# Gated copies of a token matrix: which partition holds which block of rows

## The chip, the cores and the metric

The kernel runs on one core of a Trainium2 chip. The metric is the device time in microseconds of one execution, as a median over runs. A profile of one further execution gives the engines' work in time.

## The reference

For each of 16 × 1024 = 16384 tokens there is a row `x` of 512 float32 values and 8 router logits. The two largest probabilities of the softmax over the logits are normalised to a sum of one, and the output holds the token's row twice, once scaled by each of the two (the smaller first).

```python
probs = np.exp(router_logits - logits_max)
probs = probs / np.sum(probs, axis=-1, keepdims=True)
topk_indices = np.argsort(probs, axis=-1)[..., -k:]
topk_probs = np.take_along_axis(probs, topk_indices, axis=-1)
topk_probs = topk_probs / np.sum(topk_probs, axis=-1, keepdims=True)
x_expanded = x[:, :, np.newaxis, :].repeat(k, axis=2)
return (x_expanded * topk_probs[..., np.newaxis]).astype(np.float32)
```

With two weights that sum to one, each is a sigmoid of the difference of the two largest logits. The input is 33.6 MB of `x` and 0.5 MB of logits, the output 67.1 MB.

## The kernel before

The 16384 tokens lie in 128 partitions, 128 tokens in each, in two groups: 65 tokens of each partition, then 63 (`GROUPS`). Within a group, partition p has the block of tokens 65p to 65p + 64 (or 63p to 63p + 62), which is contiguous in DRAM for `x`, for the logits and for the output. The views `x_v`, `o_v` and `rl_v` (lines 91 to 93) say so, with a rearrangement "(p m) d -> p m d".

`LOADS` says in which pieces a group's `x` is loaded into the tile `xs` (line 112): 6, 28 and 31 tokens of each partition for the first group, 32 and 31 for the second. The logits are loaded behind the first piece (lines 105 and 106), and `top2_weights` works out the weights `WA` of all tokens from them on VectorE and, for the sigmoids, ScalarE.

`STORES` is an order written out by hand. Each entry has the number of tokens of each partition, the place of the scaled rows, how many of the tokens ScalarE does, and the queue. The place is either in the tile `osp` or in `xs` itself, over tokens that have been used already. For each entry VectorE multiplies (line 127), for a few tokens ScalarE does (line 135), and one DMA stores the result (line 138). All loads and all stores but the first go through the SP queue; the first store, of two tokens, goes through ACT's. Sixteen DMAs are issued in all: five loads of `x`, two of logits, nine stores. A DMA moves one contiguous run for each partition, since a partition's tokens are neighbours in DRAM.

What waits for what follows from the tiles: a multiply waits for the load of its tokens, and for the store that last read the place it writes; a load of the second group waits for the stores that read from the same part of `xs`; a store waits for its multiply. The SP queue takes its DMAs in the order of the program, so a DMA that waits holds back those behind it.

Of the kernel before, what the change touches and what calls it, by code (L numbers as in the profile page):

```python
# [1 line left out]

# [4 lines left out]

F32 = mybir.dt.float32
ALU = mybir.AluOpType
ACTF = mybir.ActivationFunctionType  # L10
P = 128
E = 8
D = 512


GROUPS = [65, 63]
M = sum(GROUPS)


LOADS = [[6, 28, 31], [32, 31]]  # L20


STORES = [
    [
        (2, ("osp", 0), 0, "ACT"),
        (16, ("osp", 2), 0, "SP"),
        (16, ("x", 2), 0, "SP"),
        (16, ("osp", 0), 4, "SP"),
        (15, ("x", 35), 0, "SP"),
    ],  # L30
    [
        (16, ("osp", 0), 1, "SP"),
        (16, ("x", 0), 0, "SP"),
        (16, ("osp", 0), 4, "SP"),
        (15, ("x", 33), 0, "SP"),
    ],
]
OSP = 18


def top2_weights(nc, scratch, logits, WA):

    used = [0]

    def cut(n):
        a = scratch[:, used[0] : used[0] + M * n].rearrange("p (m n) -> p m n", n=n)
        used[0] += M * n
        return a

    a, b = logits[:, :, 0:4], logits[:, :, 4:8]  # L50
    hi = cut(4)
    lo = b
    nc.vector.tensor_tensor(hi, a, b, op=ALU.max)  # L53
    nc.vector.tensor_tensor(lo, a, b, op=ALU.min)  # L54
    n = 4
    while n > 1:
        n //= 2
        a, b = hi[:, :, 0:n], hi[:, :, n : 2 * n]
        nhi, nlo, tmp = cut(n), cut(n), cut(n)
        nc.vector.tensor_tensor(tmp, lo[:, :, 0:n], lo[:, :, n : 2 * n], op=ALU.max)  # L60
        nc.vector.tensor_tensor(nlo, a, b, op=ALU.min)  # L61
        nc.vector.tensor_tensor(nlo, nlo, tmp, op=ALU.max)  # L62
        nc.vector.tensor_tensor(nhi, a, b, op=ALU.max)  # L63
        hi, lo = nhi, nlo
    dlt = cut(1)
    nc.vector.tensor_tensor(dlt, hi, lo, op=ALU.subtract)  # L66
    nc.scalar.activation(WA[:, :, 0], dlt[:, :, 0], ACTF.Sigmoid, scale=-1.0)  # L67
    nc.scalar.activation(WA[:, :, 1], dlt[:, :, 0], ACTF.Sigmoid, scale=1.0)  # L68


@with_exitstack
def kernel(
    ctx: ExitStack,
    tc: tile.TileContext,
    x: bass.AP,
    router_logits: bass.AP,
    k: bass.AP,
    out: bass.AP,
):
    nc = tc.nc  # L80
    N = x.shape[0] * x.shape[1]
    assert int(k) == 2 and router_logits.shape[-1] == E and x.shape[2] == D
    assert N == P * M
    xf = x.rearrange("b s d -> (b s) d")
    of = out.rearrange("b s k d -> (b s) k d")
    rf = router_logits.rearrange("b s e -> (b s) e")
    x_v, o_v, rl_v = [], [], []
    t0 = 0
    for n in GROUPS:
        t1 = t0 + P * n  # L90
        x_v.append(xf[t0:t1].rearrange("(p m) d -> p m d", p=P))
        o_v.append(of[t0:t1].rearrange("(p m) k d -> p m k d", p=P))
        rl_v.append(rf[t0:t1].rearrange("(p m) e -> p m e", p=P))
        t0 = t1

    pool = ctx.enter_context(tc.tile_pool(name="pool", bufs=1))
    xs = pool.tile([P, max(GROUPS), D], F32)
    osp = pool.tile([P, OSP, 2, D], F32)
    WA = pool.tile([P, M, 2], F32)

    logits = osp[:, OSP - 1].rearrange("p k d -> p (k d)").rearrange("p (m e) -> p m e", e=E)
    scratch = osp[:, OSP - 3 : OSP - 1].rearrange("p r k d -> p (r k d)")

    def load_logits():
        nc.sync.dma_start(logits[:, : GROUPS[0]], rl_v[0])  # L105
        nc.sync.dma_start(logits[:, GROUPS[0] :], rl_v[1])  # L106

    m0 = 0
    for g, G in enumerate(GROUPS):
        r = 0  # L110
        for n in LOADS[g]:
            nc.sync.dma_start(xs[:, r : r + n, :], x_v[g][:, r : r + n, :])  # L112
            if g == 0 and r < 6 <= r + n:
                load_logits()
                top2_weights(nc, scratch, logits, WA)
            r += n
        assert r == G
        r = 0
        for n, (home, a), by_act, queue in STORES[g]:
            if home == "x":  # L120
                og = xs[:, a : a + 2 * n, :].rearrange("p (r k) d -> p r k d", k=2)
            else:
                og = osp[:, a : a + n]
            v = n - by_act
            w = WA[:, m0 + r : m0 + r + n, :]
            if v:
                nc.vector.tensor_tensor(  # L127
                    og[:, :v],
                    xs[:, r : r + v, :].unsqueeze(2).to_broadcast([P, v, 2, D]),
                    w[:, :v].unsqueeze(3).to_broadcast([P, v, 2, D]),  # L130
                    op=ALU.mult,
                )
            for i in range(v, n):
                for c in range(2):
                    nc.scalar.activation(  # L135
                        og[:, i, c], xs[:, r + i, :], ACTF.Copy, scale=w[:, i, c : c + 1]
                    )
            {"SP": nc.sync, "ACT": nc.scalar}[queue].dma_start(o_v[g][:, r : r + n], og)  # L138
            r += n
        assert r == G  # L140
        m0 += G


# [1 line left out]
_INS = ['x', 'router_logits', 'k']  # L145
_OUTS = [((16, 1024, 2, 512), 'float32')]

_NUMBERS = {'k': 2}


# [26 lines left out]
```

## Time and profile before

| | |
|---|---|
| median of 3 runs | 239.22 us (239.19 to 239.43) |
| profiled execution | 239.38 us, of which 237.6 us are its span (first to last instruction) |
| VectorE busy | 132.2 us |
| ScalarE busy | 13.2 us |
| moved by DMA | 101.19 MB, 426 GB/s over the span |

The profile's page gives busy times of the engines, a row of forty slices of the span with the mean busy share of the sixteen DMA engines in tenths, the DMA queues with their packets, the chain of work that ended last, and the DMAs that were issued with the time from issue to landing. A view by windows gives the DMA share and the rate of any stretch. "SPq" is the SP queue's sequencer, "L127" line 127 of the kernel. In a row such as `xs<-in_x_dram` the target stands to the left.

### The profile page before, as it was taken

The numbers are of one execution on the slowest core, as the hardware profiler recorded it, in microseconds if no ns is written. First come the engines' busy times: TensorE is split into PE (matmuls) and PEld (weight loads), VectorE is DVE, ScalarE is ACT, GpSimd is POOL, SyncE is SP. The second block draws the span as 40 slices with busy tenths as digits, with TensorE's granted clock in tenths as the row PEclk, the third lists the DMA queues.
The fourth block names the chain that finished last, engine by engine and source line by source line (L and its number), as shares of the span: only waits on it lengthen the run. The fifth ranks groups of instructions, "written<-read, shape, count | busy, mean of one in ns | idle before, by whom it ended". The sixth has DMA issues, their size and how long they took to land.

```text
span 237.6 us, 124 instructions
## 1 busy us (share of the span) xinstructions
DVE 132.2 (56%) x20; ACT 13.2 (6%) x21; POOL 0.2 (0%) x4
## 2 busy tenths in 40 slices
DVE  0640599999289999000000009999956999920000
ACT  2000000000080000000000001000006100000000
POOL 0000000000000000000000000000000000000000
DMA  7979989898989989899998989898989989897995
GB/s 265 541 338 488 408 386 535 348 530 353 496 386 441 441 353 530 353 508 414 414 519 353 508 370 502 353 519 353 496 386 419 463 353 530 353 530 342 496 445 217
DMA packets 2304, 101.19 MB, mean 426 GB/s; under 512 B 256, under 2 KB 384, under 8 KB 512
## 3 DMA queue, kind: packets, MB, share of 16 engines
q1 hardware_dynamic: 2160, 100.14, 97.7%
q10 hardware_dynamic: 144, 1.05, 1.0%
HBM read 34.08 MB, written 67.11 MB: 426 GB/s over the span
## 4 chain that ended last, share of the span: by engine, by line
DMA 48%; DVE 39%; SPq 1%; issue 0%; DVEq 0%
DMA xs<-in_x_dram 30%; DVE osp L127 25%; DMA out_dram<-osp 19%; DVE xs L127 14%; SPq L105 0%; SPq L106 0%; SPq L112 0%; SPq L138 0%; DVEq L127 0%
## 5 line engine op out<-in xcount | busy, mean ns | idle before, releaser
L127 DVE TENSOR_TENSOR osp<-xs,WA 128x12288 f32<-128x12288 f32 (+3 forms) x5 | 61.6, 12318 | 68.7 <-DMA xs<-in_x_dram 58.4
L127 DVE TENSOR_TENSOR xs<-xs,WA 128x16384 f32<-128x16384 f32 (+1 forms) x4 | 66.8, 16692 | 0.3
L135 ACT ACTIVATE osp<-xs,WA 128x512 f32<-128x512 f32 x18 | 11.4, 709 | 161.3 <-DMA out_dram<-osp 90.0
L53 DVE TENSOR_TENSOR osp<-osp 128x512 f32<-128x512 f32 x1 | 0.7, 692 | 8.2 <-DMA osp<-in_router_logits_dram 8.2
L67 ACT ACT_TABLE_LOAD x1 | 1.3, 1283 | 0.7 <-PEq L158 0.7
L67 ACT ACTIVATE WA<-osp 128x128 f32<-128x128 f32 x1 | 0.3, 316 | 10.1 <-DVE osp L66 10.1
L54 DVE TENSOR_TENSOR osp<-osp 128x512 f32<-128x512 f32 x1 | 0.7, 693 | 0.0
L60 DVE TENSOR_TENSOR osp<-osp 128x256 f32<-128x256 f32 (+1 forms) x2 | 0.7, 352 | 0.0
L62 DVE TENSOR_TENSOR osp<-osp 128x256 f32<-128x256 f32 (+1 forms) x2 | 0.7, 352 | 0.0
L63 DVE TENSOR_TENSOR osp<-osp 128x256 f32<-128x256 f32 (+1 forms) x2 | 0.7, 352 | 0.0
L61 DVE TENSOR_TENSOR osp<-osp 128x256 f32<-128x256 f32 (+1 forms) x2 | 0.7, 351 | 0.0
L66 DVE TENSOR_TENSOR osp<-osp 128x128 f32<-128x128 f32 x1 | 0.3, 292 | 0.0
L68 ACT ACTIVATE WA<-osp 128x128 f32<-128x128 f32 x1 | 0.3, 298 | 0.0
L158 POOL MEMSET const-bfloat16-1.0<- 128x1 bf16 x1 | 0.1, 102 | 0.0
L158 POOL MEMSET const-uint8-127<- 128x1 uint8 x1 | 0.1, 102 | 0.0
L158 POOL MEMSET const-float32-0.0<- 128x1 f32 x1 | 0.1, 99 | 0.2 <-issue 0.2
L158 POOL MEMSET const-float32-1.0<- 128x1 f32 x1 | 0.1, 99 | 0.0
## 6 DMA issues: line engine op xcount, KB each, us to landing
xs<-in_x_dram SPq DMA_DIRECT2D x2, 7936.0 KB, 40.8
out_dram<-xs SPq DMA_DIRECT2D x2, 7680.0 KB, 27.5
xs<-in_x_dram SPq DMA_DIRECT2D x1, 7168.0 KB, 24.2
xs<-in_x_dram SPq DMA_DIRECT2D x1, 1536.0 KB, 6.0
out_dram<-osp ACTq DMA_DIRECT2D x1, 1024.0 KB, 24.5
osp<-in_router_logits_dram SPq DMA_DIRECT2D x1, 260.0 KB, 6.2
osp<-in_router_logits_dram SPq DMA_DIRECT2D x1, 252.0 KB, 6.4
out_dram<-osp SPq DMA_DIRECT2D x4, 23.9
```

The costliest lines, as they stand in the source:

```text
L53: nc.vector.tensor_tensor(hi, a, b, op=ALU.max)
L54: nc.vector.tensor_tensor(lo, a, b, op=ALU.min)
L60: nc.vector.tensor_tensor(tmp, lo[:, :, 0:n], lo[:, :, n : 2 * n], op=ALU.max)
L61: nc.vector.tensor_tensor(nlo, a, b, op=ALU.min)
L62: nc.vector.tensor_tensor(nlo, nlo, tmp, op=ALU.max)
L63: nc.vector.tensor_tensor(nhi, a, b, op=ALU.max)
L66: nc.vector.tensor_tensor(dlt, hi, lo, op=ALU.subtract)
L67: nc.scalar.activation(WA[:, :, 0], dlt[:, :, 0], ACTF.Sigmoid, scale=-1.0)
L68: nc.scalar.activation(WA[:, :, 1], dlt[:, :, 0], ACTF.Sigmoid, scale=1.0)
L127: nc.vector.tensor_tensor(og[:, :v], xs[:, r : r + v, :].unsqueeze(2).to_broadcast([P, v, 2, D]), w[:, :v].unsqueeze(3).to_broadcast([P, v ...
L135: nc.scalar.activation(og[:, i, c], xs[:, r + i, :], ACTF.Copy, scale=w[:, i, c : c + 1])
L158: nc = _bacc.Bacc("TRN2", target_bir_lowering=False, num_devices=1)
```

## The change

The three views get one dimension more. With partition 64a + b (a of 0 or 1, b of 0 to 63), the partition now has block 2b + a of its group, where it had block 64a + b. Even blocks go to partitions 0 to 63, odd ones to 64 to 127. `x`, logits and output use the same assignment. The lines that use the views index one dimension more; tiles, pieces, queues and order stay. Lines behind 86 have numbers one higher than before.

```diff
-        x_v.append(xf[t0:t1].rearrange("(p m) d -> p m d", p=P))
-        o_v.append(of[t0:t1].rearrange("(p m) k d -> p m k d", p=P))
-        rl_v.append(rf[t0:t1].rearrange("(p m) e -> p m e", p=P))
+        x_v.append(xf[t0:t1].rearrange("(b a m) d -> a b m d", a=2, b=P // 2))
+        o_v.append(of[t0:t1].rearrange("(b a m) k d -> a b m k d", a=2, b=P // 2))
+        rl_v.append(rf[t0:t1].rearrange("(b a m) e -> a b m e", a=2, b=P // 2))
...
-            nc.sync.dma_start(xs[:, r : r + n, :], x_v[g][:, r : r + n, :])
+            nc.sync.dma_start(xs[:, r : r + n, :], x_v[g][:, :, r : r + n, :])
...
-            {"SP": nc.sync, "ACT": nc.scalar}[queue].dma_start(o_v[g][:, r : r + n], og)
+            {"SP": nc.sync, "ACT": nc.scalar}[queue].dma_start(o_v[g][:, :, r : r + n], og)
```

## The prediction

> **What bounds the kernel now.** I read the page first: the busy times, the DMA row of the forty slices, the packet count and the queues.
>
> ```profile
> span 237.6 us, 124 instructions
> ...
> DVE 132.2 (56%) x20; ACT 13.2 (6%) x21; POOL 0.2 (0%) x4
> ...
> DMA  7979989898989989899998989898989989897995
> ...
> DMA packets 2304, 101.19 MB, mean 426 GB/s; under 512 B 256, under 2 KB 384, under 8 KB 512
> ## 3 DMA queue, kind: packets, MB, share of 16 engines
> q1 hardware_dynamic: 2160, 100.14, 97.7%
> q10 hardware_dynamic: 144, 1.05, 1.0%
> HBM read 34.08 MB, written 67.11 MB: 426 GB/s over the span
> ```
>
> VectorE works 132.2 us of 237.6. The sixteen DMA engines are busy 97.7% + 1.0% = 98.7% of the span, from the first slice to the last, so the transfers set the time: about 0.987 × 237.6 = 234.5 us of work for each of the sixteen engines and 3.1 us in which they stand idle, at the start and behind the last landing. The view by windows gives the rate in stretches.
>
> ```profile
> 0.00:10.00 10.00, 1.81 (x4) 1.28 (x1) 0.20 (x4) 1.00 0.98 393
> 26.00:44.00 18.00, 17.61 (x2) 0.00 (x0) 0.00 (x0) 1.00 1.02 442
> 142.00:180.00 38.00, 33.38 (x2) 1.34 (x2) 0.00 (x0) 1.00 1.01 435
> ...
> 26.00:236.00 210.00, 126.07 (x8) 11.36 (x18) 0.00 (x0) 1.00 1.00 431
> ```
>
> The last two columns are the DMA share and GB/s. From 26 to 236 us all sixteen engines are always busy (1.00) and move 431 GB/s, 26.9 GB/s for each engine. The chain of waits is divided between DMA and VectorE:
>
> ```profile
> DMA 48%; DVE 39%; SPq 1%; issue 0%; DVEq 0%
> DMA xs<-in_x_dram 30%; DVE osp L127 25%; DMA out_dram<-osp 19%; DVE xs L127 14%; SPq L105 0%; SPq L106 0%; SPq L112 0%; SPq L138 0%; DVEq L127 0%
> ```
>
> Its 39% of VectorE isn't a second limit: a multiply is followed by its store, but other transfers fill the engines meanwhile, which the share of 1.00 shows.
>
> **How a transfer is spread now.** This is what the change touches. The list of DMA issues:
>
> ```profile
> xs<-in_x_dram SPq DMA_DIRECT2D x2, 7936.0 KB, 40.8
> out_dram<-xs SPq DMA_DIRECT2D x2, 7680.0 KB, 27.5
> xs<-in_x_dram SPq DMA_DIRECT2D x1, 7168.0 KB, 24.2
> xs<-in_x_dram SPq DMA_DIRECT2D x1, 1536.0 KB, 6.0
> out_dram<-osp ACTq DMA_DIRECT2D x1, 1024.0 KB, 24.5
> osp<-in_router_logits_dram SPq DMA_DIRECT2D x1, 260.0 KB, 6.2
> osp<-in_router_logits_dram SPq DMA_DIRECT2D x1, 252.0 KB, 6.4
> out_dram<-osp SPq DMA_DIRECT2D x4, 23.9
> out_dram<-xs SPq DMA_DIRECT2D x2, 24.1
> xs<-in_x_dram SPq DMA_DIRECT2D x1, 46.4
> ```
>
> These are 16 DMAs, and 2304 packets are 144 for each: 128 with data, one for each partition, and 16 more. The 256 packets under 512 B are the 16 × 16 small ones, since the shortest run of data is a partition's logits, 252 KB / 128 = 2016 B. I read the 16 as one completion for each engine that took part: every DMA was cut into 16 parts of 8 partitions.
>
> **The change part by part.** The instructions of both kernels stand in the same order on every engine; only the DMAs' patterns differ. One load and one store of each, DRAM side beside SBUF side, as they are built:
>
> ```
> before  load   x    [128][3072]          xs   [128][3072]
> after   load   x    [2][64][3072]        xs   [128][1][3072]
> before  store  out  [128][16384]         osp  [128][16384]
> after   store  out  [2][64][16384]       osp  [128][1][16384]
> ```
>
> Bytes, contiguous runs (one for each partition, 2016 B to 64 KB) and partitions stay as they are. No compute instruction is added, removed or moved, and no wait. In DRAM, partition 64a + b now steps two blocks for each b and one for a; the two steps can't be merged into one, so the outermost count on the DRAM side is 2 in all 16 DMAs. The unknown is into how many parts such a DMA is cut, and the trace, where both sides always begin with 128, has no row with another count. The bounds:
>
> - Sixteen parts as now: the 234.5 us for each engine stay, and the time is 239.38 us, that of the profiled execution.
> - Two parts, one for each value of the outermost count: the packets' time is 16 × 234.5 = 3752 engine-us, so 1876 us on each of two engines. By the rate it is the same: 101.19 MB / (2 × 26.9 GB/s) = 1880 us.
>
> I take two. In this trace the parts are equal and made of whole partitions (16 × 8 = 128), a cut along the first dimension of both patterns. With 2 on one side and 128 on the other, no more than two equal parts can be cut along both. For sixteen, the cut would have to go through the first dimension on the one side and the second on the other, and no row shows that it can.
>
> [...]
>
> The sum: 1876 us of packets, plus the same 3.1 us of idle start and end, is a span of 1879 us; plus 239.38 - 237.6 = 1.8 us around the span, 1881 us. The median of the runs, 239.22, is 0.16 us below the profiled execution, which doesn't matter here.
>
> This holds if the two engines never run dry. VectorE's work doesn't grow:
>
> ```profile
> L127 DVE TENSOR_TENSOR xs<-xs,WA 128x16384 f32<-128x16384 f32 x2 | 34.5, 17225 | 0.1
> ...
> L127 DVE TENSOR_TENSOR osp<-xs,WA 128x12288 f32<-128x12288 f32 x2 | 25.9, 12958 | 9.8 <-DMA out_dram<-osp 9.8
> ```
>
> A multiply takes at most 17.2 us, and each big transfer, at 53.9 GB/s, 136 us (7168 KB) to 156 us (a store of 16 rows, 8.39 MB). In each place where the kernel waits, one such transfer is still under way: the first big multiply waits for the 7168 KB load while the 7936 KB load follows; the third store's buffer waits for the second to land while the third is already queued (counting the small store as the first); the second group's first load is queued behind two stores, and its first multiply runs while its second load moves. That second load is the closest call, since SP holds it back until the last store of the first group has landed:
>
> ```profile
> SPq L112 <- DMA out_dram<-xs: 26.2, 1, 26.2
> ```
>
> It is issued when the first load of that group, ahead of it, has just begun, with some 156 us to go. So the waits become longer but stay covered: nothing is added. Were this cover gone, each of the eight big multiplies would add up to 17.2 us, 138 us in all.
>
> The issue is on the path once:
>
> ```profile
> 0.73 0.38 SPq L112
> ```
>
> A pattern of more dimensions may take longer to issue; no row shows by how much. Between 0 and a doubling that is up to 0.4 us at the start, and I take 0: the later issues stand in front of a full queue.
>
> **The rivals.**
>
> *Sixteen parts after all* (the change does nothing to the spread): this is the case that is not slower. [...] For it speaks that the partitions are still 128 and the parts can be made of the same 128 runs; against it, that the patterns no longer start alike. The time is 239.4 us. Other addresses then meet at the same moment in DRAM, to either side; with 3.1 us idle in all, a gain can't pass 1.3%, and there is no row from which to price a loss.
>
> *Two engines, each faster.* If the 26.9 GB/s were the share of a limit common to all sixteen, two alone could draw more. At twice the rate: 1876 / 2 + 4.9 = 943 us. Against it: the share is 1.00 with 431 GB/s over loads, stores and mixtures of both, which looks like an engine's own pace. No row has few engines at work.
>
> *One engine, or two in each other's way.* If the whole DMA went to one engine, or the two had to share a path, 3752 + 4.9 = 3757 us. For it speaks only that the trace never shows two engines alone; against it, that 2 divides both 2 and 128.
>
> **How the numbers follow.** Two engines at the present rate: 82%. Sixteen: 12%, of which 3% faster, 5% the same, 4% slower. Two engines clearly faster: 3%. One engine, or half the rate: 3%. The likeliest time is 1881 us. Its own bounds are rates that rows show: the fastest stretch, 442 GB/s, makes 101.19 MB / (442 / 8) + 4.9 = 1836 us; the first ten us, with 393 GB/s at a share of 0.98 (401 GB/s at full share, small and first packets among them), make 101.19 MB / (401 / 8) + 4.9 = 2024 us. The range of 1830 to 2025 us leaves out the other cases, 18% in all. A measurement of this kernel can tell about 0.2% from no change. Slower by more than that: 82 + 4 + 3 + 3 = 92%; within it 5%; faster 3%.
>
> **What would show it.** In the changed kernel's profile I expect a mean DMA share near 2/16 (0.12 to 0.13) through the span, about 54 GB/s, the same 101.19 MB, and 16 × (128 + 2) = 2080 packets, 32 of them under 512 B. The 7936 KB load would move in about 151 us when alone. VectorE's multiplies keep their 13.0 and 17.2 us, 132.2 us in sum, and idle between them grows; the chain becomes nearly all DMA. The forecast is wrong if the packets stay 2304 with a share near 0.99 (sixteen parts), if the share is 2/16 but the rate far from 54 GB/s (the pace isn't the engine's own), or if the share falls well under 2/16 in the middle of the span (the cover by queued transfers fails).

## The result

The changed kernel takes 1871.3 us (median of 4 runs, 1871.29 to 1871.57), the kernel before 239.2 us (239.16 to 239.43). The ratio is 7.818, with a 95% interval of 7.808 to 7.827. Here and below, a median and its range are of all runs of a kernel, and a ratio with an interval is of the runs within 1.5% of its fastest. The forecast was 1881 us, with a range of 1830 to 2025.

The page of the changed kernel, with the parts that were read of the kernel before (span, busy times, share of the DMA engines and GB/s in forty slices, packets, queues, and the chain that ended last):

```profile
span 1869.5 us, 124 instructions
## 1 busy us (share of the span) xinstructions
DVE 132.2 (7%) x20; ACT 13.2 (1%) x21; POOL 0.2 (0%) x4
...
DMA  1111111111111111111111111111111111111111
GB/s 50 55 54 56 54 54 54 55 53 53 56 53 53 56 53 53 56 54 55 53 55 56 53 53 54 54 54 56 53 53 56 53 55 55 53 56 53 55 53 53
DMA packets 2080, 101.19 MB, mean 54 GB/s; under 512 B 32, under 2 KB 160, under 8 KB 288
## 3 DMA queue, kind: packets, MB, share of 16 engines
q1 hardware_dynamic: 1950, 100.14, 12.4%
q10 hardware_dynamic: 130, 1.05, 0.1%
...
another core or an unknown queue 68%; DVE 7%; DMA 2%; SPq 0%; issue 0%; ACT 0%; DVEq 0%
```

The same 101.19 MB move and VectorE has the same 132.2 us, but the DMA row, which was 7 to 9 in all slices but the last, is 1 everywhere. The shares of 12.4% and 0.1% make 12.5%, which is two engines of sixteen, busy all the time. There are 32 small packets where there were 256: two completions for each of 16 DMAs. The chain can't put a name to its longest part, and the page's list of DMA issues has no times to landing for this run; that the profile can't match two completions to their DMA is a guess. The program has one core, so that these 68% are not another core's. The waits show what they are:

```profile
DVE osp L128 <- DMA xs<-in_x_dram: 725.8, 2, 579.2
...
DVE osp L128 <- DMA out_dram<-osp: 541.9, 2, 271.2
```

The first big multiply of each group waits for a load and the third for a store, at the same places as before (58.4 and 9.8 us in the kernel before). The two rows add up to 1267.7 us, which is 68% of the span.

### The profile page after: what moved, and what is told of

Same layout as the page of the kernel before. It is cut to its first block, busy times and chain, and to the rows that moved or that the text cites. A ratio compares the mean times of both kernels' runs of the same rounds, so it can differ in the third digit from the quotient of the medians.

```text
span 1869.5 us, 124 instructions
## 1 busy us (share of the span) xinstructions
DVE 132.2 (7%) x20; ACT 13.2 (1%) x21; POOL 0.2 (0%) x4
## 2 busy tenths in 40 slices
DMA packets 2080, 101.19 MB, mean 54 GB/s; under 512 B 32, under 2 KB 160, under 8 KB 288
## 3 DMA queue, kind: packets, MB, share of 16 engines
q1 hardware_dynamic: 1950, 100.14, 12.4%
## 4 chain that ended last, share of the span: by engine, by line
another core or an unknown queue 68%; DVE 7%; DMA 2%; SPq 0%; issue 0%; ACT 0%; DVEq 0%
DVE xs L128 4%; DVE osp L128 3%; DMA osp<-in_router_logits_dram 2%; DVE osp L53 0%; DVE osp L54 0%; SPq L113 0%; DVE osp L62 0%; DVE osp L63 0%; DVE osp L61 0%; DVE osp L60 0%; SPq L106 0%; ACT WA L67 0%; DVE osp L66 0%; ACT WA L68 0%
```

## The experiments

Two questions stood behind the forecast: does the outermost count of 2 alone do this, or does the new order of blocks in DRAM have a part in it; and is 27 GB/s an engine's own pace, so that the number of engines is all that matters?

### The new assignment without the 2

Each DMA is issued as two, one for each a, with 64 partitions on both sides:

```diff
+    H = P // 2
...
+    def halves(engine, dst, src, dram_is_src):
+        for a in range(2):
+            p = slice(a * H, (a + 1) * H)
+            engine.dma_start(dst[p] if dram_is_src else dst[a], src[a] if dram_is_src else src[p])
...
-            nc.sync.dma_start(xs[:, r : r + n, :], x_v[g][:, :, r : r + n, :])
+            halves(nc.sync, xs[:, r : r + n, :], x_v[g][:, :, r : r + n, :], True)
```

> The new assignment of blocks to partitions, with each DMA written as two DMAs of 64 partitions (one for each a), so that 64 stands outermost on both sides. Theory (the outermost count of 2 limits a DMA to two engines): 16 parts again, about 239 us, between 237 and 243 since the 32 DMAs double the issues and the completions; 32 x (64 + 16) = 2560 packets. Rival (the new addresses, the order of the blocks over partitions, are what is slow): the time stays near 1871 us.

Measured: 445.6 us (median of 6, 435.8 to 452.2). Neither expectation holds: sixteen engines are back, but at about half the rate.

```profile
span 443.1 us, 153 instructions
...
DMA packets 2560, 101.19 MB, mean 228 GB/s; under 512 B 512, under 2 KB 640, under 8 KB 768
## 3 DMA queue, kind: packets, MB, share of 16 engines
q1 hardware_dynamic: 2400, 100.14, 95.9%
```

The 512 small packets are 32 × 16, and the engines are busy 97% of the span (with the 0.8% of the other queue); but they move 228 GB/s where they moved 426, so a packet takes nearly twice as long. So a second effect exists, and the next runs had to say whether it comes from the order in DRAM, from the partitions or from the smaller DMAs.

### Other counts outermost

The same edit with 16, 8 and 4 for the 2 (here 16):

```diff
-        x_v.append(xf[t0:t1].rearrange("(b a m) d -> a b m d", a=2, b=P // 2))
+        x_v.append(xf[t0:t1].rearrange("(b a m) d -> a b m d", a=16, b=P // 16))
```

> Partition 8a + b has block 16b + a (a of 16, b of 8): the DRAM side begins with 16, still three dimensions, 16 DMAs. Theory: 16 parts, about 239 us (238 to 241), 2304 packets. Rival (any DMA whose DRAM side has three dimensions loses its spread, whatever the first count): near 1871 us with 2080 packets. Rival (addresses in a strided order cost by themselves): above 245 us at 2304 packets.

Measured: 443.3 us (median of 6, 439.8 to 448.3); the ratio to the kernel before is 1.845, interval 1.840 to 1.851. The 2304 packets are as predicted, so the third dimension doesn't cost the spread, but the time is no nearer to 239 us: here, too, sixteen engines run at about half the rate (231 GB/s at a share of 1.01 from 50 to 150 us, 244 at 0.99 from 280 to 420 us). The number alone would suit the rival of strided addresses; the runs with 32 and 64 outermost, below, have strided addresses and the time of the full rate (239.75 and 239.89 us).

> Partition 16a + b has block 8b + a: the DRAM side begins with 8. Theory: eight parts at 27.1 GB/s for each engine, 101.19 MB / (8 x 27.1) = 467 us and about 3 us around it, 470 us; packets 16 x (128 + 8) = 2176, DMA share 0.50. If the pace were a share of a common limit, eight engines would draw more than 27.1 GB/s each and end below 440 us.

Measured: 784.5 us (one run, as for all below that name no median), a miss; 2176 packets and a share of 0.48 (47.4% and 0.5%), so eight engines, as expected, but slower ones.

> Partition 32a + b has block 4b + a: the DRAM side begins with 4. Theory: four parts, 101.19 MB / (4 x 27.1) = 933 us and about 3 us around it, 937 us; packets 16 x (128 + 4) = 2112, DMA share 0.25. With a common limit: below 900 us.

Measured: 1118.7 us, a miss in time again, with the 2112 packets of four engines. The windows of this run show how. The last two columns are the share of the sixteen engines and GB/s:

```profile
200.00:280.00 80.00, 0.00 (x0) 0.00 (x0) 0.00 (x0) 1.00 0.25 64
300.00:400.00 100.00, 0.00 (x0) 0.00 (x0) 0.00 (x0) 1.00 0.24 69
400.00:500.00 100.00, 29.11 (x2) 5.01 (x8) 0.00 (x0) 1.00 0.25 83
500.00:600.00 100.00, 0.00 (x0) 0.00 (x0) 0.00 (x0) 1.00 0.25 105
600.00:1100.00 500.00, 62.50 (x4) 6.35 (x10) 0.00 (x0) 1.00 0.25 109
```

Four engines are always busy, at 64 GB/s early and 109 GB/s from 600 us on, which is 27 GB/s for each. The kernel didn't change in between. Something slows the engines at first and lets go later. What it is isn't shown: no trace shows where an engine is, and the runs below test only which partitions matter. With eight engines the rate doesn't recover for good. Two windows of the run with 8 outermost:

```profile
400.00:550.00 150.00, 33.38 (x2) 1.33 (x2) 0.00 (x0) 1.00 0.50 148
550.00:650.00 100.00, 29.12 (x2) 5.01 (x8) 0.00 (x0) 1.00 0.49 133
```

Eight engines at 27 GB/s would move 217.

### The old assignment in halves

Partition p has block p, as before the change; each DMA is cut at partition 64.

```diff
+    PARTS = [(0, 64), (64, 128)]
...
+        for p0, p1 in PARTS:
+            engine.dma_start(dst[p0:p1], src[p0:p1])
```

> The assignment of before (partition p has block p), with each DMA cut in two of 64 partitions, 0 to 63 and 64 to 127; 2560 packets. [...]

If the new order of blocks in DRAM were what halves the rate, halves in the old order would run at the full one. Measured: 448.7 us (median of 4, 445.6 to 449.1), ratio 1.870, interval 1.863 to 1.877. Blocks in their old order are as slow in halves as the new ones (445.6), within the 4% by which the runs of those scatter. So the order in DRAM isn't what halves the rate; whether the partitions or the smaller DMAs do is for the next run. But for the last two, the slices lie between 179 and 327 GB/s:

```profile
GB/s 179 255 188 269 217 216 250 226 246 235 240 205 223 211 235 252 205 251 247 221 260 205 199 209 222 199 217 327 264 270 270 205 229 258 240 230 245 242 165 27
```

The packets' own times show where the rate goes. Of the 1536 packets over 50 KB, 997 moved at 12 to 14 GB/s, half of the 27 GB/s that 1495 of them have in the kernel before.

### The same cut in another place

```diff
-    PARTS = [(0, 64), (64, 128)]
+    PARTS = [(32, 96), (0, 32), (96, 128)]
```

> The assignment of before, with each DMA cut in three: partitions 32 to 95, 0 to 31, 96 to 127; 3 x 16 x 16 completions and 2048 packets with data, 2816. [...] Rival (a DMA of 64 partitions is slow whichever they are, by its smaller parts): 443 us or more.

Measured: 382.5 us, well below 443. There are more and smaller DMAs than in halves, and still it is 66 us faster. The slices show bursts that halves never have:

```profile
GB/s 219 483 220 231 449 220 209 420 275 255 413 248 234 393 261 322 349 317 301 247 212 223 241 213 223 342 317 227 337 255 179 227 324 260 266 234 228 129 103 26
```

Slices of 393 to 483 GB/s stand among others near 220, in the first half about one in three, as if the pieces from 32 to 95 and the pieces of 32 partitions took turns; the slices don't name the piece. A piece from 32 to 95 is as large as a half and as contiguous in DRAM, so it differs from a half in its partitions, and neither in size nor in lying in one stretch of DRAM. The last slices fall to 129, 103 and 26 GB/s.

### Two outermost, without interleaving

```diff
-    xf = x.rearrange("b s d -> (b s) d")
+    xf = x.rearrange("b s d -> (b s) d").rearrange("(a t) d -> a t d", a=2)
...
-        x_v.append(xf[t0:t1].rearrange("(b a m) d -> a b m d", a=2, b=P // 2))
+        x_v.append(xf[:, t0:t1].rearrange("a (b m) d -> a b m d", b=P // 2))
```

> The DRAM side begins with 2 as in the changed kernel, but without interleaving: partitions 0 to 63 have the first half of all tokens, in order, and 64 to 127 the second half. Theory (the outermost count alone decides): two engines, 2080 packets, 1871 us within 5. Rival (the interleaved order of blocks has a share in it): at least 1% less.

Measured: 1871.4 us, beside 1871.3 of the changed kernel. With blocks in order and the 2 outermost, the whole loss is there.

### Two engines on partitions 32 apart

The changed kernel's pattern on 64 partitions at a time, so that the two values of the outermost count stand for partitions 32 apart instead of 64 apart:

```diff
-        x_v.append(xf[t0:t1].rearrange("(b a m) d -> a b m d", a=2, b=P // 2))
+        x_v.append(xf[t0:t1].rearrange("(b h a m) d -> h a b m d", h=2, a=2, b=P // 4))
...
+        for h in range(2):
+            p = slice(h * (P // 2), (h + 1) * (P // 2))
+            engine.dma_start(dst[p] if dram_is_src else dst[h], src[h] if dram_is_src else src[p])
```

> Each DMA cut in two of 64 partitions, and the DRAM side of each begins with 2: one engine moves partitions 0 to 31 while the other moves 32 to 63, then 64 to 95 beside 96 to 127; 32 x (64 + 2) = 2112 packets. [...] Rival (two engines always have 54 GB/s): 1875 us.

Measured: 2124.7 us, 250 us over the 1875 of two engines at 54 GB/s throughout. Windows of this run:

```profile
60.00:290.00 230.00, 0.54 (x1) 0.00 (x0) 0.00 (x0) 1.00 0.12 35
300.00:540.00 240.00, 28.10 (x2) 0.00 (x0) 0.00 (x0) 1.00 0.12 32
560.00:740.00 180.00, 0.00 (x0) 0.00 (x0) 0.00 (x0) 1.00 0.12 40
800.00:2100.00 1300.00, 62.50 (x4) 6.35 (x10) 0.00 (x0) 1.00 0.13 54
```

Two engines, always busy, move 32 to 40 GB/s in the windows up to 740 us and 54 GB/s from 800 us on. In the changed kernel, with the two 64 partitions apart, the slices show 50 to 56 GB/s throughout. The cut into halves, which this run has and the changed kernel hasn't, is there in the late windows too, at the full 54 GB/s. So two busy engines can be slow for a time, and since the order in DRAM (1871.3 and 1871.4 us) and the cut (54 GB/s late in this run) make no such difference, the partitions are what is left to decide whether they are.

### One direction alone

The views of the change for the loads alone (the output rows then stand in another order), and for the stores alone.

```diff
-        o_v.append(of[t0:t1].rearrange("(b a m) k d -> a b m k d", a=2, b=P // 2))
+        o_v.append(of[t0:t1].rearrange("(p m) k d -> p m k d", p=P))
```

> The new views for x and the logits alone, the stores as before (so the output rows stand in another order than the reference's). Theory: the loads run on two engines, the stores on sixteen; each of the two engines has 34.08 / 2 + 67.11 / 16 = 21.2 MB at 27.1 GB/s, 783 us, and the time is 780 to 800 us. Packets 7 x 130 + 9 x 144 = 2206.

Measured: 789.8 us, as expected, with the 2206 packets.

> The new view for the output alone, the loads as before (output rows in another order). Theory: each of the two engines has 67.11 / 2 + 34.08 / 16 = 35.7 MB, 1317 us, and some 25 us before the stores flow: 1335 to 1355 us. Packets 9 x 130 + 7 x 144 = 2178. Were the DRAM side of a load not what counts (only that of a store), this would come near 1871 us and the run with the loads alone near 239.

Measured: 1324.1 us, 11 us under the range: the 25 us for the start were too many, since all sixteen engines load at first (a share of 0.97 and 414 GB/s in the first 40 us). The 1317 us of the two engines' bytes alone are 0.5% off. A count of 2 on the DRAM side acts alike whether DRAM is read or written. The slices of the run with the loads alone show both rates in one execution:

```profile
GB/s 46 52 103 52 58 52 52 58 52 57 418 418 71 52 58 52 52 60 286 410 189 53 53 53 53 53 57 57 52 318 424 165 58 52 52 58 53 146 420 312
```

### Full spread with interleaved blocks

> Partition 4a + b has block 32b + a: the DRAM side begins with 32. Theory (at most 16 parts, in the order of the outermost dimension): each engine has the same eight neighbouring partitions as with 16, so 2304 packets and 435 to 455 us. Rival (the order of blocks in DRAM sets the time): a time other than that of the 16.

Measured: 239.75 us. My expectation of how rows are handed out was wrong, and so was its rival's reason: with 32 outermost the engines work at full rate (425 GB/s, 426 before).

```profile
span 238.0 us, 124 instructions
...
DMA packets 2304, 101.19 MB, mean 425 GB/s; under 512 B 256, under 2 KB 384, under 8 KB 512
## 3 DMA queue, kind: packets, MB, share of 16 engines
q1 hardware_dynamic: 2160, 100.14, 97.5%
```

Blocks interleaved by 32 cost nothing that one run can tell. The last kernel has 64 outermost, and was run more often:

> Partition 2a + b has block 64b + a: the DRAM side begins with 64. [...] If the order of blocks in DRAM cost anything at full rate, it would show as more than 240.5 us at the same packets.

Measured: 239.89 us (median of 7, 239.63 to 240.11) beside 239.26, ratio 1.0026, interval 1.0015 to 1.0038. Part of the 0.6 us that are left has a place at the start, where the engines have nothing to do. The timeline of this run (start, duration, engine, line):

```profile
0.73 0.67 SPq L113 DMA_DIRECT2D xs<-in_x_dram  x1
1.45 0.58 SPq L106 DMA_DIRECT2D osp<-in_router_logits_dram  x1
2.08 0.60 SPq L107 DMA_DIRECT2D osp<-in_router_logits_dram  x1
```

The first issue takes 0.67 us where it took 0.38, and in this trace the last multiply starts 0.26 us later than before (at 193.52 and 193.26 us), so nothing is added in between. The traced execution took 239.65 us; what the slower ones add isn't traced.

## Why the forecast was right

**Two parts.** The step on which everything rested, that an outermost count of 2 on the DRAM side leaves two parts, holds: 2080 packets, 32 of them small, a share of 12.5%. Before the result it was the author's estimate: the trace before, with 128 first on both sides, shows sixteen parts and no other number. Counts of 4 and 8 gave the packets of four and eight engines (2112 and 2176), 16 and 32 those of sixteen (2304), and 64 the time of sixteen (239.89 us). The block order had no part: 1871.3 interleaved, 1871.4 in order.

**The engine's own pace.** Two engines move 54 GB/s where sixteen moved 431: 27 GB/s each in both, and the same for four in the late windows above (109 GB/s). The rival of two faster engines falls.

**The sum.** Predicted were 1879 us of span and 1.8 us around it; measured 1869.5 and 1.8. The term that was mis-sized, by 0.5%, is the packets' time together with the idle start and end: 101.19 MB over the measured span are 27.06 GB/s for each of two engines, and the forecast's 1876 us of packets are 26.97 GB/s, with 3.1 us of idle on top. The page gives the shares to 0.1%, some 15 us for two engines, too coarse to divide these 9.5 us further.

**The cover.** "So the waits become longer but stay covered" holds: the share is 0.12 to 0.13 in every window of 200 us and more, and the multiplies add nothing. In the windows of the changed kernel:

```profile
200.00:400.00 200.00, 30.98 (x2) 0.00 (x0) 0.00 (x0) 1.00 0.12 54
400.00:800.00 400.00, 29.12 (x2) 5.01 (x8) 0.00 (x0) 1.00 0.13 54
800.00:1200.00 400.00, 33.38 (x2) 1.34 (x2) 0.00 (x0) 1.00 0.13 54
```

One wait came that the forecast didn't have. It let only the second load of the second group wait for a store; here both do:

```profile
SPq L113 <- DMA out_dram<-xs: 272.4, 2, 147.8
```

The closest call came out as it was reckoned. The second load was issued at 956.0 us, and the multiply behind the first started at 1110.7: 155 us to go, against the 156 of the forecast.

**What the forecast didn't see.** It gave "two in each other's way" 3% together with one engine, and argued against it only that 2 divides both counts. That wasn't a reason. With the two parts of a DMA 32 partitions apart, two engines were slower (2124.7 us, 32 to 40 GB/s at first); in the change the parts are 64 apart, and the slices show 50 to 56 GB/s throughout. That the change's two engines fell on the better side of this was luck: nothing in the forecast told the two cases apart. And the rival of sixteen parts was priced at 239.4 us, which holds for some divisions (239.75 and 239.89 with 32 and 64 outermost) but not for others: sixteen parts with 16 outermost take 443.3 us, and in halves 445.6. The forecast was right on its main line, but its idea that only the number of parts counts was incomplete.

Why halves (448.7 us), 16 outermost (443.3) and the pair 32 apart (2124.7) are slow, while the cut at 32 and 96 (382.5) is less so and 32 and 64 outermost (239.75 and 239.89) are not, isn't shown beyond this: the partitions matter. No run shows which engine took which partition, and none has 16 outermost with the blocks in order, so that for 16 the order in DRAM isn't ruled out by itself.

## What to carry to other kernels

Look at the first dimension of both access patterns of a DMA as built, not at the number of partitions: a permutation of blocks that only seems to rename addresses can leave a small count there and with it a few engines (here 2, and two engines). A small count of packets under 512 B (32 where there were 256) and a flat low DMA share (0.12 to 0.13) show it on one page. A count of 16 engaged all engines here (2304 packets) but not at their full rate: 32, 64 and 128 ran at full rate (239.75, 239.89 and 239.2 us), 16 and two halves at about half of it (443.3 and 448.7 us).

## What the runs showed of the hardware that was not expected

With the parts of a DMA 32 partitions apart, the engines ran slowly at first and recovered by themselves: from 32 to 54 GB/s with two engines over some 800 us, and with the four of the run with 4 outermost from 64 to 109 over 600 us. With two, stores of the first group are what moves from 560 to 980 us (an estimate from the bytes that the windows add up to), so it isn't the kind of transfer that changes. Eight engines (148, then 133 of 217 GB/s) and sixteen in halves (226 of 426 over the span) don't recover within their runs. Why some do and others don't is open.

The issue of a DMA took up to 102 us when the transfers ahead were spread over two engines, where a store's took 0.33 to 0.37 us in the kernel before. In the timeline of the changed kernel:

```profile
2.05 27.32 SPq L107 DMA_DIRECT2D osp<-in_router_logits_dram  x1
29.41 10.30 SPq L113 DMA_DIRECT2D xs<-in_x_dram  x2
...
231.04 101.96 SPq L139 DMA_DIRECT2D out_dram<-xs  x1
```

SP is held for 27.3 us by the third DMA, which took 0.6 us in the run with 64 outermost. With two engines each has 65 packets of a DMA instead of 9. Other runs lie between. The third to fifth DMA with 4 outermost (33 packets of each for an engine), then the fourth and fifth with 8 (17 packets):

```profile
2.10 0.53 SPq L107 DMA_DIRECT2D osp<-in_router_logits_dram  x1
2.67 23.60 SPq L113 DMA_DIRECT2D xs<-in_x_dram  x2
...
2.85 1.24 SPq L113 DMA_DIRECT2D xs<-in_x_dram  x2
```

With two engines the first two DMAs, 130 packets for each engine, take 0.69 and 0.53 us to issue, and the third is held. With four, the first three make 99, and none takes more than 0.71 us; the fourth and fifth, which bring it to 165, take 23.60 us together. With eight, all five make 85, and the last two take 1.24 us together. So issues were held where more packets for each engine stood ahead; what holds them, and from which count on, no run measured. The forecast had priced an issue at no more than 0.8 us. The hold cost nothing here, since the two engines had work the whole time (a share of 0.13 in the first 200 us and 0.12 to 0.13 in all windows behind), but a queue that is held for 102 us would matter to a kernel whose SP queue has anything urgent behind.
